# A gated hybrid decoder layer on one core: first operands loaded in another order and four pieces of work moved

## The chip, the cores and the metric

The kernel runs on one core of a Trainium2 chip, in one launch. The metric is the device time in microseconds (us), as the median of several runs; lower is better. The profile is one execution recorded by the hardware profiler. Engines: PE (TensorE) multiplies, DVE (VectorE) and ACT (ScalarE) work on elements, POOL (GpSimd) does a few small steps, SP (SyncE) issues DMA transfers.

## What is computed

One layer of a decoder, for 512 tokens of width 1024, all in float32:

```python
h  = rmsnorm(x, g_mix)
z  = h @ w_in                 # retention q,k,v,gate; 3 attention groups q,k,v; 2 merge gates
A  = silu(rg) * rmsnorm(retention(rotate(rq), rotate(rk), rv))        # 4 heads, chunks of 128
Bt = merge of 3 groups: dilated_window_attention(rotate(norm(aq)), rotate(norm(ak)), av)
x  = x + (sig(g_A) * (A @ w_ret_out) + sig(g_B) * (Bt @ w_att_out)) @ w_o
x  = x + relu(rmsnorm(x) @ w_up)**2 @ w_down
x  = x + sig(rmsnorm(x) @ w_ple_gate) * (p @ w_ple_proj)
```

The three attention groups are merged by their softmax denominators: each head's output is a sum over groups of a weight per token times the group's output.

## The kernel before, in words

**Products in three parts.** Each float32 factor is split into a high part that PE takes fast and a low part (the rest). A product is then three matmuls: high by high, high by low, low by high. The tile names carry this: `whi` and `wlo` are the parts of a weight unit, `hh` and `hl` those of the activations. `split_unit` (line 223) makes the two parts of a weight unit of 256 x 512: the high part on ACT (line 237), the rest on DVE (line 238). `mm3` (line 246) issues the three matmuls (lines 249 to 251), 128 x 128 by 128 x 512 each.

**Weights.** `make_plan` (line 1164) lists all weight units in the order of use. `fetch` issues their DMAs on SP (line 200) into six raw buffers; `ahead(n)` (line 205) fetches and splits so that n units lie ready past the used ones; `units(n)` (line 217) hands out n units and calls `ahead` for two more.

**A row projection** (`rows_gemm`, line 253) has eight k blocks of 128 channels, two weight units at a time, and four token tiles t of 128. For each t and each unit six matmuls run; then `tick` (line 115) moves a clock on by one, so a projection of 96 matmuls has 16 ticks. `later(lag, fn)` queues work that is let out `lag` ticks later, at most two entries every second tick, in the order of the queue among those that are due. So transposes, scores and merging are put between the matmuls of projections. `force(key)` lets entries out until the named one is done.

**Order of instructions.** Outside marked stretches a planner orders each engine's instructions. Within `manual_schedule` ACT and DVE keep program order: that holds for the query and key projections of the first attention group (lines 659 to 662) and for the tail. Instructions marked with `keep_in_program_order` keep theirs too. DMAs on SP are ordered by the planner everywhere.

**The start** (`setup`, line 377; `first_panel`, line 441). `x_cols` is x transposed: eight tiles of 128 channels x 512 tokens. On SP, tiles of x and of the first weights alternate (lines 388 and 391), 256 KB each. The very first weights come in two halves, one on ACT's queue and one on SP's (lines 393 and 394). The gains' columns `gcol` come first on ACT's queue (line 382). Seven matmuls on zeros warm PE up (line 411). Each x tile is scaled by its gain into `hh` on ACT (line 449) and into `hl` on DVE (line 450); the very first `whi` is made by DVE (line 233). The first k block is multiplied in rounds: for all four t high by high (line 468), then low activations (line 470), then low weights (line 472). From k = 1 on each t has its three products in a row by `mm3`. The last four k blocks run t by t, and each finished t is consumed.

**The first query projection** (`att_proj(0, 0)`, line 580, the lazy case). It runs without the norm of x; after the last t it works out the token factors, then a factor per token and head (`factor`, line 611: DVE, then a power on POOL, line 614) and multiplies the rotated tiles by it (`scale`, line 616, on DVE, line 618). `tables` (line 569) multiplies rotation rows and gains on DVE (line 573). `heads_T` (line 552) queues the transposes of the rotated tiles, one head an entry (line 559).

**Later work of interest.** After each attention group's projections, `scores`, `transpose4` and `values` are queued. After the third group `merge` (line 722) is queued: a chain of small DVE and ACT steps makes a weight for every token, group and head; the weights are gathered in `cw` (line 754), transposed on PE (line 756), copied by ACT, written to DRAM (line 760), and loaded back as rows spread over all partitions (line 766). `weigh` (line 768) multiplies each head's group output by its row (line 771) and adds (line 776); after a head's third group the sum is split into `oh` and `ol` (lines 780 and 781). The twelve steps are queued, and the mix (line 922), far behind, forces them. `ret_proj` (line 796) makes the retention keys: copy, rotation and decay per t, then `heads_T` with a lag of 9.

Of the kernel before, what the change touches and what calls it, by code (L numbers as in the profile page):

```python
# [14 lines left out]
ALU = mybir.AluOpType  # L15
AX = mybir.AxisListType

P = 128
# [58 lines left out]
class Block:  # L77
# [299 lines left out]
    def setup(self):  # L377
        nc, a = self.nc, self.a
        self.gcol = self.const.tile([P, 48], F32, name="gcol")
        xr = [self.big("xr") for _ in range(2)]  # L380
        self.x_cols = [xr[k // 4][:, k % 4] for k in range(KD)]
        nc.scalar.dma_start(self.gcol, a["vec_cols"])
        for u in range(KD // 2):
            src, _ = self.plan[u]
            raw = self.wraw.tile([P, 1024], F32, tag="raw", name=self.nm("raw")).rearrange("p (k n) -> p k n", k=2)
            for k in range(2):
                c = slice((2 * u + k) * P, (2 * u + k + 1) * P)
                nc.sync.dma_start(self.x_cols[2 * u + k], a["x_cols"][c])
                w = src[k * P : (k + 1) * P]
                if u or k:  # L390
                    nc.sync.dma_start(raw[:, k], w)
                else:
                    nc.scalar.dma_start(raw[: P // 2, k], w[: P // 2])
                    nc.sync.dma_start(raw[P // 2 :, k], w[P // 2 :])
            self.raws.append((raw, None))
        self.load_tables()
        self.fetch(6)
        self.x_tiles = []
        xb = [self.big("x") for _ in range(2)]
        for t in range(NT):  # L400
            v = xb[t // 2].rearrange("p (t c) n -> p t (c n)", t=2)[:, t % 2]
            nc.sync.dma_start(v, a["x"][0, t * P : (t + 1) * P])
            self.x_tiles.append(v)
        self.ident = self.const.tile([P, P], F32, name="ident")
        make_identity(nc, self.ident)
        warm = self.tmp("warm")
        nc.vector.memset(warm, 0.0)
        nc.scalar.activation(warm[:, 500:501], warm[:, 501:502], AF.Copy)
        wb, wps = warm.bitcast(mybir.dt.bfloat16), self.bank("warm")
        for _ in range(WARM):  # L410
            nc.tensor.matmul(wps, wb[:, :P], wb[:, :512], start=True, stop=True)
        self.mhalf = self.const.tile([P, H], F32, name="mhalf")
        nc.gpsimd.memset(self.mhalf, -0.5)
# [18 lines left out]
        self.nc.sync.dma_start(self.gains[:, g0:g1].rearrange("p g n e -> p (g n e)"),  # L432
                               bass.AP(tensor=g.tensor, offset=g.offset + w * g0, ap=[[0, P], [1, w * (g1 - g0)]]))

    def load_rest(self):
        self.nc.sync.dma_start(self.mask, self.a["c_mask"])
        self.gain_rows(1, NG)
        self.rot_rows(1)


    def first_panel(self, consume, tables):
        nc = self.nc
        self.hT = self.new_act(2, "h")
        us = []

        def split_x(k):
            g = self.gcol[:, k : k + 1]
            h, l = (part[k // 4][:, k % 4] for part in self.hT)
            self.pin(nc.scalar.activation(R(h), self.x_cols[k], AF.Copy, scale=g))
            nc.vector.scalar_tensor_tensor(R(l), self.x_cols[k], g, h, op0=ALU.mult, op1=ALU.subtract)  # L450

        self.pinned = True
        for u in range(KD // 2):
            self.hook = lambda i: split_x(2 * u + i)
            us += self.units(1)
        self.hook = None
        self.pinned = False
        banks = [self.gbank() for _ in range(NT)]

        def part(t, k):  # L460
            wh, wl = us[k // 2]
            sh, sl = self.stat(self.hT, k, t, False)
            self.mm3(banks[t], sh, sl, wh[:, k % 2], wl[:, k % 2], k == 0, k == KD - 1)

        (wh, wl), mm = us[0], nc.tensor.matmul
        parts = [self.stat(self.hT, 0, t, False) for t in range(NT)]
        for t, (sh, _) in enumerate(parts):
            mm(banks[t], sh, wh[:, 0], start=True, stop=False)
        for t, (_, sl) in enumerate(parts):
            mm(banks[t], sl, wh[:, 0], start=False, stop=False)  # L470
        for t, (sh, _) in enumerate(parts):
            mm(banks[t], sh, wl[:, 0], start=False, stop=False)
        for k in range(1, KD // 2):
            for t in range(NT):
                part(t, k)
        tables()
        self.ready_tabs = self.tables(0, 1)
        for t in range(NT):
            for k in range(KD // 2, KD):
                part(t, k)  # L480
            consume(t, banks[t])
            if t == 1:
                self.pinned = True
                self.ahead(2)
                self.pinned = False
            self.tick()
# [82 lines left out]
    def tables(self, g, n):  # L569
        C = self.tabp.tile([P, NT, HD], F32, tag="tab", name=self.nm("C"))  # L570
        Sn = self.tabp.tile([P, NT, HD], F32, tag="tab", name=self.nm("S"))
        for o, part, gi in ((C, 0, 2 * n), (Sn, 1, 2 * n + 1)):
            ins = self.nc.vector.tensor_tensor(
                o, self.rc[:, 0, :, part * HD : (part + 1) * HD],
                self.gains[:, g, gi].unsqueeze(1).to_broadcast([P, NT, HD]), op=ALU.mult)
            if g == 0:
                self.tc.keep_in_program_order(ins)
        return C, Sn

    def att_proj(self, g, n):  # L580
# [5 lines left out]
        def consume(t, ps):  # L586
            ss, v, r = self.small(H, "ss"), self.small(H, "v"), self.small(H, "r")
            j = self.tmp("j")
            for h in range(H):
                c = slice(h * HD, (h + 1) * HD)  # L590
                nc.scalar.activation(j[:, c], ps[:, c], AF.Square, accum_out=ss[:, h : h + 1])
            C, Sn = tabs[0]
            rots.append(self.rotate(ps, C[:, t], Sn[:, t]))
            sums.append((ss, v, r))
            if not lazy:
                factor(t)
                if t:
                    scale(t - 1)
                if t == NT - 1:
                    scale(t)  # L600
            elif t == NT - 2:
                self.token_squares(0)
            elif t == NT - 1:
                self.token_squares(2)
                self.token_factors()
                for i in range(NT):
                    factor(i)
                for i in range(NT):
                    scale(i)

# [45 lines left out]
    def attention(self, g):  # L656
        nc = self.nc
        if g == 0:
            with self.tc.manual_schedule(engines={nc.scalar.engine, nc.vector.engine}):
                qT = self.att_proj(g, 0)  # L660
                kT = self.att_proj(g, 1)
                self.load_rest()
        else:
            qT, kT = self.att_proj(g, 0), self.att_proj(g, 1)
        v = self.v_proj(g > 0)
        oT = self.big("oT")
        st = self.const.tile([P, NT, 2, H], F32, name=f"st{g}")

# [53 lines left out]
    def merge(self, groups, oh, ol):  # L722
# [29 lines left out]
        wide = self.tmp("cw")[:, : NG * H * NT]  # L752
        for g in range(NG):
            nc.vector.tensor_copy(wide[:, g * H * NT : (g + 1) * H * NT].rearrange("p (h r) -> p r h", h=H), cs[g])
        ps = self.bank("pc")
        nc.tensor.transpose(ps[: NG * H * NT, :P], wide, self.ident)
        turned = self.tmp("ct")[: NG * H * NT, :P]
        nc.scalar.activation(turned, ps[: NG * H * NT, :P], AF.Copy)
        cd = self.dram.tile([NG * H, S], F32, name="c_dram", tag="c_dram")
        nc.sync.dma_start(cd.rearrange("a (r l) -> (a r) l", r=DIL), turned)  # L760
        accs, spread = [None] * H, {}
        nat = lambda ap: ap.rearrange("p (l r) -> p r l", r=DIL)

# [4 lines left out]
        def weigh(h, g):  # L768
# [7 lines left out]
            nc.vector.tensor_tensor(n, accs[h], t, op=ALU.add)  # L776
            accs[h] = n
            if g == NG - 1:
                av = n.rearrange("p (r l) -> p r l", r=DIL)
                nc.scalar.activation(R(nat(oh[:, h])), av, AF.Copy)  # L780
                nc.vector.tensor_tensor(R(nat(ol[:, h])), av, nat(oh[:, h]), op=ALU.subtract)

        items = [(h, g) for h in range(H) for g in range(NG)]
        for i, (h, g) in enumerate(items):
            if i == 0:
                for p in items[:3]:
                    self.later(4, lambda p=p: load(*p))

            def step(i=i, h=h, g=g):
                weigh(h, g)  # L790
                if i + 3 < len(items):
                    load(*items[i + 3])
            self.later(8, step, ("O", h, g))


    def ret_proj(self, extra=None):
# [7 lines left out]
                extra(t, rots[t])  # L804

        self.rows_gemm(self.hT, KD, consume)
        return self.heads_T(rots, False, 9)

    def ret_cols(self):

# [111 lines left out]
    def mix(self, A, O):  # L922
        nc = self.nc
        U, Z = [[None] * 4, [None] * 4], {}
        for pair in ((0, 2), (1, 3)):
            parts = {}
            for br, act, nk, bo in (("a", O, H, 24), ("r", A, KD, 16)):
                if pair[0] and br == "r":
                    self.load_x()
                for cc in pair:  # L930
# [32 lines left out]
                    for h in range(H):  # L963
                        if br == "a":
                            self.force(("O", h, NG - 1))
                        else:
                            for i in range(NT):
                                self.force(("A", h, i))
# [216 lines left out]
    def run(self):  # L1185
# [4 lines left out]
        for g in range(NG):  # L1190
            groups.append(self.attention(g))
        oh, ol = self.big("oh"), self.big("ol")
        self.later(12, lambda: self.merge(groups, oh, ol))
        A = self.retention()
        mx = self.mix(A, ([oh], [ol]))
        self.tail(mx)
# [29 lines left out]
```

## Time and profile before

| | |
|---|---|
| Median of 3 runs | 998.5 us (998.46 to 999.19) |
| Profiled execution, its own time | 997.21 us |
| Span from first to last instruction in it | 995.4 us, so 1.8 us lie around it |
| Mean granted clock of PE | 1.000 |
| DMA in the span | 141.15 MB, 142 GB/s in the mean |

In a row of the waits stand the waiting engine with the tile it writes and its line, the releaser, the us in total, the times, and the longest. In a row of the timeline stand the start, the duration, engine, line, operation, tiles, shapes and the count of merged instructions, and in brackets the idle time before and what ended it. Matmuls are pipelined: an instruction's duration is longer than the step to the next one, so the pace is read from starts. In a DMA row stand the count, the size and the median time from issue to landing. In a row of groups stand the count, the busy time in us, the mean ns of one and the idle time before. A row of windows gives the stretch, its length, the busy time of PE, PE's weight loads, DVE, ACT and POOL, the granted clock, the DMA share and GB/s.

### The profile page before, as it was taken

The page shows a single profiled execution, that of the slowest core. Times are in us where ns is not written, and L with a number is a line of the kernel's source. Part 1 is how long each engine was busy: PE and PEld are TensorE (multiplying, and loading weights), DVE is VectorE, ACT ScalarE, POOL GpSimd, SP SyncE. Part 2 cuts the span into 40 slices and gives each one's busy share as a digit, 9 for nine tenths or more (in the row PEclk, how much of TensorE's full clock was granted, in tenths as well). Part 3 has the DMA queues.
Part 4 walks back from the last instruction along what each step waited for, and adds up shares of the span by engine and source line. Part 5 has one row for each costly group of instructions (what it writes and reads, how often), then busy time and mean ns, then how long its engine had stood idle before and what let it go on. Part 6 is the DMA issues. An engine that isn't in the chain of part 4 may idle for free.

```text
span 995.4 us, 12449 instructions
## 1 busy us (share of the span) xinstructions
PE 984.7 (99%) x4588; PEld 826.1 (83%) x4588; DVE 647.6 (65%) x1014; ACT 461.8 (46%) x938; POOL 97.4 (10%) x98
## 2 busy tenths in 40 slices
PE   8999999999999999999999999999999999999998
PEld 6788899889887888888888878888888888888886
DVE  6866675774878344554643696668667759766953
ACT  5535344433433334342422447764564565465451
POOL 0210220220000010001002010110101001000000
PEclk9999999999999999999999999999999999999999
DMA  9632132323353312222346496758659766875911
GB/s 337 240 101 76 54 106 85 105 76 106 93 142 120 113 43 85 86 85 85 132 146 166 125 233 193 190 128 225 179 136 212 203 167 153 238 160 131 312 54 53
DMA packets 90781, 141.15 MB, mean 142 GB/s; under 512 B 6320, under 2 KB 40416, under 8 KB 90720
## 3 DMA queue, kind: packets, MB, share of 16 engines
q1 hardware_dynamic: 79616, 119.22, 37.5%
q0 software_dynamic: 10880, 20.97, 12.7%
q8 instruction: 36, 0.59, 0.2%
q10 hardware_dynamic: 224, 0.16, 0.1%
q14 instruction: 25, 0.20, 0.1%
HBM read 136.10 MB, written 4.24 MB: 141 GB/s over the span
## 4 chain that ended last, share of the span: by engine, by line
PE 94%; DVE 4%; issue 1%; DMA 0%; ACT 0%; POOL 0%; ACTq 0%; DVEq 0%; POOLq 0%
PE pg L251 25%; PE pg L250 25%; PE pg L249 25%; PE pb L251 3%; PE pb L249 3%; PE pb L250 3%; PE po L700 1%; PE ph L559 1%; PE pt L325 1%; PE sc L677 1%; DVE wlo L238 1%; PE ry L899 1%; PE pe L651 1%; PE kv L887 1%; PE sc L683 1%
## 5 line engine op out<-in xcount | busy, mean ns | idle before, releaser
L238 DVE TENSOR_TENSOR wlo<-raw,whi 128x1024 fp32r<-128x1024 f32 (+1 forms) x166 | 196.8, 1191 | 103.8 <-ACT whi L237 101.8
L237 ACT ACTIVATE whi<-raw 128x1024 fp32r<-128x1024 f32 (+1 forms) x165 | 169.5, 1032 | 195.3 <-PE pg L251 75.4
L249 PE MATMUL pg<-whi,hh 128*128 128x512 f32 x444 | 178.6, 402 | 0.0
L250 PE MATMUL pg<-wlo,hh 128*128 128x512 f32 x444 | 173.6, 391 | 1.0 <-DVE wlo L238 1.0
L251 PE MATMUL pg<-whi,hl 128*128 128x512 f32 x444 | 173.7, 391 | 0.0
L250 PEld LDWEIGHTS pg<-wlo,hh 128*128 128x128 f32 x444 | 91.4, 206 | 15.3 <-DVE wlo L238 1.4
L251 PEld LDWEIGHTS pg<-whi,hl 128*128 128x128 f32 x444 | 91.1, 205 | 15.1
L249 PEld LDWEIGHTS pg<-whi,hh 128*128 128x128 f32 x444 | 91.3, 206 | 14.0
L249 PE MATMUL pg<-h2h,whi 128*128 128x512 f32 x256 | 99.6, 389 | 0.0
L250 PE MATMUL pg<-h2l,whi 128*128 128x512 f32 x256 | 99.6, 389 | 0.0
L251 PE MATMUL pg<-h2h,wlo 128*128 128x512 f32 x256 | 99.6, 389 | 0.0
L242 ACT ACTIVATE whi<-raw,gcol 128x256 fp32r<-128x256 f32 (+1 forms) x144 | 66.1, 523 | 21.3 <-PE pg L250 12.4
L243 DVE SCALAR_TENSOR_TENSOR wlo<-raw,gcol,whi 128x256 fp32r<-128x256 f32 (+1 forms) x144 | 65.5, 510 | 15.6 <-ACT whi L242 15.6
L202 POOL DMA_DIRECT2D raw<-in_w_down x32 | 38.6, 1206 | 302.4 <-DMA raw<-in_w_down 147.8
L249 PE MATMUL pg<-hh,whi 128*128 128x512 f32 x160 | 64.0, 400 | 0.0
L249 PE MATMUL pg<-whi,uh 128*128 128x512 f32 x160 | 62.8, 392 | 0.0
L251 PE MATMUL pg<-whi,ul 128*128 128x512 f32 x160 | 62.6, 392 | 0.0
L250 PE MATMUL pg<-wlo,uh 128*128 128x512 f32 x160 | 62.4, 390 | 0.0
L251 PE MATMUL pg<-hh,wlo 128*128 128x512 f32 x160 | 62.4, 390 | 0.0
L250 PE MATMUL pg<-hl,whi 128*128 128x512 f32 x160 | 62.3, 390 | 0.0
L250 PEld LDWEIGHTS pg<-h2l,whi 128*128 128x128 f32 x256 | 48.0, 188 | 10.0
L251 PEld LDWEIGHTS pg<-h2h,wlo 128*128 128x128 f32 x256 | 48.0, 188 | 10.0
(201 smaller groups left out, 1685.2 us busy)
## 6 DMA issues: line engine op xcount, KB each, us to landing
raw<-in_w_in SPq DMA_DIRECT2D x72, 512.0 KB, 4.1
raw<-in_w_down SPq DMA_DIRECT2D x48, 512.0 KB, 4.3
raw<-in_w_up SPq DMA_DIRECT2D x32, 512.0 KB, 5.2
raw<-in_w_down POOLq DMA_DIRECT2D x32, 512.0 KB, 6.7
raw<-in_w_o SPq DMA_DIRECT2D x12, 512.0 KB, 4.3
x<-in_x SPq DMA_DIRECT2D x8, 512.0 KB, 7.1
raw<-in_w_ret_out SPq DMA_DIRECT2D x8, 512.0 KB, 3.5
raw<-in_w_o POOLq DMA_DIRECT2D x8, 512.0 KB, 5.8
```

The costliest lines, as they stand in the source:

```text
L202: self.nc.gpsimd.dma_start(raw, rows(add[0]), accum_op=ALU.add)
L237: self.pin(nc.scalar.activation(R(hi[:, i]), raw[:, i], AF.Copy))
L238: nc.vector.tensor_tensor(R(lo[:, i]), raw[:, i], hi[:, i], op=ALU.subtract)
L242: self.pin(nc.scalar.activation(R(hi[:, i]), raw[:, i], AF.Copy, scale=g))
L243: nc.vector.scalar_tensor_tensor(R(lo[:, i]), raw[:, i], g, hi[:, i], op0=ALU.mult, op1=ALU.subtract)
L249: t.matmul(ps, sh, mh, start=first, stop=False, skip_group_check=more)
L250: t.matmul(ps, sh, ml, start=False, stop=False, skip_group_check=more)
L251: t.matmul(ps, sl, mh, start=False, stop=last, skip_group_check=more)
L325: nc.tensor.transpose(ps[:, k * P : (k + 1) * P], part[:, k * P : (k + 1) * P], self.ident)
L559: self.nc.tensor.transpose(ps[:, t * P : (t + 1) * P], rots[t][:, h * HD : (h + 1) * HD], self.ident)
L651: self.nc.tensor.transpose(ps[:, k * P : (k + 1) * P], e[:, k * P : (k + 1) * P], self.ident)
L677: nc.tensor.matmul(sc[:, h * P : (h + 1) * P], qT[:, h, rs], kT[:, h, rs], start=True, stop=True)
```

## The change

1. In `setup`, the first x tile is loaded in halves of 256 tokens, and the first weights come in one piece on SP between them. ACT's queue no longer carries weights.
2. In `first_panel`, the first x tile is scaled in halves; k blocks 0 and 1 are both multiplied in rounds.
3. In the lazy query projection, `ahead(4)` is called between the factors and the scalings.
4. `load_rest` goes: the mask is loaded after the first group's key projection, the other gains and the second rotation rows after its value projection.
5. `tables` keeps program order for all groups.
6. `merge` is queued with lag 20 instead of 12. In it, the transpose of the weights with the copy and the write behind it is an entry of its own four ticks later; the loads come at 6 instead of 4 and the steps at 10 instead of 8. The split of each head's sum becomes an entry four ticks behind its last step, which the mix forces as well.
7. The transposes of the retention keys have a lag of 14 instead of 9.

```diff
             for k in range(2):
                 c = slice((2 * u + k) * P, (2 * u + k + 1) * P)
-                nc.sync.dma_start(self.x_cols[2 * u + k], a["x_cols"][c])
-                w = src[k * P : (k + 1) * P]
-                if u or k:
-                    nc.sync.dma_start(raw[:, k], w)
-                else:
-                    nc.scalar.dma_start(raw[: P // 2, k], w[: P // 2])
-                    nc.sync.dma_start(raw[P // 2 :, k], w[P // 2 :])
+                first = u == 0 and k == 0
+                x = lambda i: nc.sync.dma_start(self.x_cols[2 * u + k][:, i], a["x_cols"][c, i])
+                x(slice(0, 256) if first else slice(0, S))
+                nc.sync.dma_start(raw[:, k], src[k * P : (k + 1) * P])
+                if first:
+                    x(slice(256, S))
...
-            self.pin(nc.scalar.activation(R(h), self.x_cols[k], AF.Copy, scale=g))
-            nc.vector.scalar_tensor_tensor(R(l), self.x_cols[k], g, h, op0=ALU.mult, op1=ALU.subtract)
+            for c in (slice(0, 256), slice(256, S)) if k == 0 else (slice(0, S),):
+                self.pin(nc.scalar.activation(R(h[:, c]), self.x_cols[k][:, c], AF.Copy, scale=g))
+                nc.vector.scalar_tensor_tensor(R(l[:, c]), self.x_cols[k][:, c], g, h[:, c], op0=ALU.mult, op1=ALU.subtract)
...
-        parts = [self.stat(self.hT, 0, t, False) for t in range(NT)]
-        for t, (sh, _) in enumerate(parts):
-            mm(banks[t], sh, wh[:, 0], start=True, stop=False)
...
-        for k in range(1, KD // 2):
+        for k in range(2):
+            parts = [self.stat(self.hT, k, t, False) for t in range(NT)]
+            for t, (sh, _) in enumerate(parts):
+                mm(banks[t], sh, wh[:, k], start=k == 0, stop=False)
+            for t, (_, sl) in enumerate(parts):
+                mm(banks[t], sl, wh[:, k], start=False, stop=False)
+            for t, (sh, _) in enumerate(parts):
+                mm(banks[t], sh, wl[:, k], start=False, stop=False)
+        for k in range(2, KD // 2):
...
-            if g == 0:
-                self.tc.keep_in_program_order(ins)
+            self.tc.keep_in_program_order(ins)
...
                 for i in range(NT):
                     factor(i)
+                self.ahead(4)
                 for i in range(NT):
                     scale(i)
...
-                self.load_rest()
+            self.nc.sync.dma_start(self.mask, self.a["c_mask"])
...
         v = self.v_proj(g > 0)
+        if g == 0:
+            self.gain_rows(1, NG)
+            self.rot_rows(1)
...
-        ps = self.bank("pc")
-        nc.tensor.transpose(ps[: NG * H * NT, :P], wide, self.ident)
...
+        def turn():
+            ps = self.bank("pc")
+            nc.tensor.transpose(ps[: NG * H * NT, :P], wide, self.ident)
+            turned = self.tmp("ct")[: NG * H * NT, :P]
+            nc.scalar.activation(turned, ps[: NG * H * NT, :P], AF.Copy)
+            nc.sync.dma_start(cd.rearrange("a (r l) -> (a r) l", r=DIL), turned)
+
+        self.later(4, turn)
...
+                def split():
+                    av = n.rearrange("p (r l) -> p r l", r=DIL)
+                    nc.scalar.activation(R(nat(oh[:, h])), av, AF.Copy)
+                    nc.vector.tensor_tensor(R(nat(ol[:, h])), av, nat(oh[:, h]), op=ALU.subtract)
+
+                self.later(4, split, ("split", h))
...
-                    self.later(4, lambda p=p: load(*p))
+                    self.later(6, lambda p=p: load(*p))
...
-            self.later(8, step, ("O", h, g))
+            self.later(10, step, ("O", h, g))
...
-        return self.heads_T(rots, False, 9)
+        return self.heads_T(rots, False, 14)
...
                             self.force(("O", h, NG - 1))
+                            self.force(("split", h))
...
-        self.later(12, lambda: self.merge(groups, oh, ol))
+        self.later(20, lambda: self.merge(groups, oh, ol))
```

More of the change, by code (lines that the diff above doesn't have):

```diff
@@ L433, in gain_rows @@
                                bass.AP(tensor=g.tensor, offset=g.offset + w * g0, ap=[[0, P], [1, w * (g1 - g0)]]))
[L435 to L438, printed above, removed]
     def first_panel(self, consume, tables):
@@ L465, in first_panel @@
         (wh, wl), mm = us[0], nc.tensor.matmul
-        parts = [self.stat(self.hT, 0, t, False) for t in range(NT)]
-        for t, (sh, _) in enumerate(parts):
[L468 to L472, printed above, removed]
-        for k in range(1, KD // 2):
+        for k in range(2):
[7 more added lines that the diff above has]
+        for k in range(2, KD // 2):
             for t in range(NT):
@@ L754, in merge @@
             nc.vector.tensor_copy(wide[:, g * H * NT : (g + 1) * H * NT].rearrange("p (h r) -> p r h", h=H), cs[g])
-        ps = self.bank("pc")
-        nc.tensor.transpose(ps[: NG * H * NT, :P], wide, self.ident)
-        turned = self.tmp("ct")[: NG * H * NT, :P]
-        nc.scalar.activation(turned, ps[: NG * H * NT, :P], AF.Copy)
         cd = self.dram.tile([NG * H, S], F32, name="c_dram", tag="c_dram")
-        nc.sync.dma_start(cd.rearrange("a (r l) -> (a r) l", r=DIL), turned)
+        def turn():
[5 more added lines that the diff above has]
+        self.later(4, turn)
         accs, spread = [None] * H, {}
@@ L778, in weigh @@
             if g == NG - 1:
-                av = n.rearrange("p (r l) -> p r l", r=DIL)
-                nc.scalar.activation(R(nat(oh[:, h])), av, AF.Copy)
-                nc.vector.tensor_tensor(R(nat(ol[:, h])), av, nat(oh[:, h]), op=ALU.subtract)
+                def split():
[3 more added lines that the diff above has]
+                self.later(4, split, ("split", h))
         items = [(h, g) for h in range(H) for g in range(NG)]
```

## The prediction

> **What bounds the kernel now.** I began with the page's first part, then took the waits of PE alone.
>
> ```profile
> span 995.4 us, 12449 instructions
> ...
> PE 984.7 (99%) x4588; PEld 826.1 (83%) x4588; DVE 647.6 (65%) x1014; ACT 461.8 (46%) x938; POOL 97.4 (10%) x98
> ```
> ```profile
> PE pg L468 <- DVE whi L233: 1.9, 1, 1.9
> PE warm L411 <- DVE warm L407: 1.5, 1, 1.5
> PE ph L559 <- DVE ro L549: 1.2, 1, 1.2
> PE pg L250 <- DVE wlo L238: 1.0, 1, 1.0
> PE pc L756 <- DVE cw L754: 0.8, 1, 0.8
> ```
>
> PE works in 99% of the span, so an edit pays only where PE stands still, and the second view lists every such place: the wait for the first operands and three single waits for DVE. (The warm-up's own wait comes before any data and stays.) The change touches all four; what it can win is their sum, and what it can lose is a new entry in this list. PE's starts in order of time give the size of each gap.
>
> ```profile
> 1.46 3.17 PE L411 MATMUL warm<-warm 128*128 128x512 bf16 x7 [1.46 <-DVE warm L407]
> 6.53 1.17 PE L468 MATMUL pg<-whi,hh 128*128 128x512 f32 x4 [1.90 <-DVE whi L233]
> ...
> 9.35 0.39 PE L249 MATMUL pg<-whi,hh 128*128 128x512 f32 x1
> ```
>
> The first k, twelve matmuls, takes 6.53 to 9.35: 2.82 us, 0.235 each. That is PE's pace, and whatever starts it earlier moves everything behind it.
>
> **The start.** Five views: the chain's first wait, the DMA issues and their time to landing, the queue of SP, then DVE and ACT.
>
> ```profile
> 1.19 4.74 DMA raw<-in_w_in
> ```
> ```profile
> xr<-in_x_cols SPq DMA_DIRECT2D x1, 256.0 KB, 3.0
> raw<-in_w_in SPq DMA_DIRECT2D x1, 128.0 KB, 3.1
> raw<-in_w_in ACTq DMA_DIRECT2D x1, 128.0 KB, 4.7
> gcol<-in_vec_cols ACTq DMA_DIRECT2D x1, 24.0 KB, 3.2
> ```
> ```profile
> raw<-in_w_in SPq DMA_DIRECT2D x2, 256.0 KB, 4.8
> ```
> ```profile
> 1.18 0.55 SPq L394 DMA_DIRECT2D raw<-in_w_in  x1
> 1.78 0.57 SPq L388 DMA_DIRECT2D xr<-in_x_cols  x1
> ```
> ```profile
> 5.96 0.43 DVE L233 CAST whi<-raw 128x512 fp32r<-128x512 f32 x1 [4.56 <-DMA raw<-in_w_in]
> ...
> 8.23 0.68 DVE L238 TENSOR_TENSOR wlo<-raw,whi 128x512 fp32r<-128x512 f32 x1
> ```
> ```profile
> 3.96 0.72 ACT L449 ACTIVATE hh<-xr,gcol 128x512 fp32r<-128x512 f32 x1 [0.69 <-DMA gcol<-in_vec_cols]
> 6.44 0.72 ACT L449 ACTIVATE hh<-xr,gcol 128x512 fp32r<-128x512 f32 x1 [1.76 <-DMA xr<-in_x_cols]
> 7.10 0.63 ACT L237 ACTIVATE whi<-raw 128x512 fp32r<-128x512 f32 x1
> ```
>
> The two halves of the first weights leave within 0.01 us of each other, SP's at 1.18 and ACT's at 1.19, but SP's lands after 3.1 us (4.3) and ACT's after 4.74 (5.93). DVE's cast starts at 5.96 and PE at 6.53, so the first matmul follows the last landing by 0.60 us. In the new form all the weights go on SP behind half of x. Up to their last byte SP has then moved 128 + 256 KB, the same 384 KB as 256 + 128 KB now. Lower bound of their landing: 1.18 + 3.1 = 4.3. Upper bound: the next 256 KB pieces of this queue need 4.8, which gives 6.0 and no gain. I take 4.6, near the lower end, because the row nearest in size, place and bytes ahead is the 3.1 us one; the 0.3 is for a larger transfer. The first matmul is then at 4.6 + 0.6 = 5.2, a gain of **1.3 us** (bounds 1.6 and -0.1).
>
> [...]
>
> Is anything else late at 5.2? ACT's first scaling waits until 3.96 for the gains' columns, as before, and half a tile costs at most the 0.72 of a whole one: done by 4.7. The second half of x is issued where the second x tile is now, at 1.78, with half its bytes; at 3.1 us it lands at 4.9 and is scaled by 5.6. PE wants it with the third matmul, 5.2 + 2 x 0.235 = 5.7. That is tight, with no stall in the sum; its bad case is a rival. DVE gets one more instruction, at most 0.7, behind a cast that runs 1.3 earlier. ACT's queue loses one DMA issue and SP keeps its count.
>
> The next k is wanted at 5.2 + 2.82 = 8.0. Its whi is ready at 7.10 + 0.63 = 7.73 and its wlo at 8.23 + 0.68 = 8.91, neither counted as earlier. In the old order of products wlo is the second operand wanted, at 8.2: a stall of 0.7. In rounds it is wanted eight matmuls later, at 9.9. So the rounds cost nothing and protect the gain.
>
> **The wait at 39 us.** PE, then DVE:
>
> ```profile
> 39.27 0.39 PE L249 MATMUL pg<-whi,hh 128*128 128x512 f32 x1
> 40.66 0.50 PE L250 MATMUL pg<-wlo,hh 128*128 128x512 f32 x1 [1.00 <-DVE wlo L238]
> ```
> ```profile
> 34.06 0.63 DVE L613 TENSOR_SCALAR v<-ss,floor 128x4 f32<-128x4 f32 x4
> 35.86 0.69 DVE L618 TENSOR_TENSOR ro<-ro,r 128x512 f32<-128x512 f32 x1 [1.17 <-POOL r L614]
> ...
> 39.39 3.49 DVE L238 TENSOR_TENSOR wlo<-raw,whi 128x1024 fp32r<-128x1024 f32 x3
> ```
>
> The step from 39.27 to 40.66 is 1.39 us against 0.235: 1.16 lost. DVE works in program order here; four scalings wait one by one for POOL, and the weights PE needs are split only from 39.39. With the added call two weight units (L238, 3.49/3 = 1.16 each) stand ahead of the scalings: 34.69 to 37.0, two units before PE asks. Part of that fills the 1.17 in which DVE is idle now. The scalings then find their factors made and end at about 37.0 + 4 x 0.69 = 39.8, against 39.4; their readers, the head transposes, are sixteen ticks away. Gain **1.16 us**, 0 if the raw weights were late, which ACT's split of them does not show.
>
> **The wait at 265 us.**
>
> ```profile
> 265.21 0.39 PE L251 MATMUL pg<-hh,wlo 128*128 128x512 f32 x1
> 266.37 0.27 PE L756 MATMUL pc<-ident,cw 128*48 128x128 f32 x1 [0.77 <-DVE cw L754]
> ```
>
> 1.16 less 0.235: 0.93 lost, because the transpose of the group weights is put on PE in the same tick as the DVE chain that makes its input. Four ticks of six matmuls, 4 x 6 x 0.235 = 5.6 us, now lie between them. Gain **0.93 us**, less about 0.15 for one more break in the stream of matmuls (an estimate: the first matmul after this stretch's transposes needs a load that the 0.235 pace otherwise hides).
>
> **The wait at 309 us.**
>
> ```profile
> 308.47 0.71 PE L559 MATMUL ph<-ident,ro 128*128 128x128 f32 x5
> 310.38 0.55 PE L559 MATMUL ph<-ident,ro 128*128 128x128 f32 x3 [1.20 <-DVE ro L549]
> ```
> ```profile
> L771 DVE TENSOR_TENSOR mt<-oT,cb 128x512 f32<-128x512 f32 x12 | 8.2, 696 | 0.8 <-ACT oT L151 0.8
> ...
> L781 DVE TENSOR_TENSOR ol<-mt,oh 128x512 fp32r<-128x512 f32 x4 | 4.4, 1095 | 1.4 <-ACT oh L780 1.4
> ```
> ```profile
> 312.00:334.00 22.00, 22.00 (x103) 18.30 (x102) 11.42 (x13) 8.87 (x10) 0.00 (x0) 1.00 0.34 104
> ```
>
> The last rotated tile of the retention keys is late because DVE weighs the attention groups among the rotations. I count **1.2 us**, the listed wait. The transposes move five ticks (7 us) later, and the weighing starts eight plus two ticks (14 us) later, so it leaves most of the rotations. That weighing is 8.2 + 4.4, and eight additions at about 0.7, 5.6: 18.2 us of DVE. It goes into the next projection, where the last row has DVE at 11.42 of 22. Four ticks of delay of each split have no cost: its reader, the mix, is far behind.
>
> **The small moves.** Mask, gains and rotation rows leave SP's early stretch for places where their first readers (masking of scores, tables of the second group, retention keys) are still tens of microseconds off. The tables of later groups stay in order on DVE, four products less among the early ones. Taken at nothing; if the gains were late, DVE would stop ahead of the second group's weights, bounded by one SP transfer, 4.8 us.
>
> **Sum.** 1.3 + 1.16 + 0.93 + 1.2 - 0.15 = 4.4, rounded up to 4.6 for the slow steps right behind each wait (0.50 against 0.39 at 40.66, the same at the start). The profiled execution, 997.21, becomes 992.6. It lies 1.3 under the shown median, 998.5, so the forecast is **993.9**.
>
> **Rivals.**
> - *A new wait of DVE takes the place of one removed*: order outside the written-out stretches is a planner's, and 14 us later other work crosses. Price: one wait like those listed, 1.2 to 1.4. For: three such waits stand now. Against: DVE's room in the row above. 995.2.
> - *The second half of x gates*: if it takes 4.7 to 4.8 like the later pieces, it lands at 6.5, is scaled by 7.2, and PE's third matmul starts no sooner than now. The start gains nothing: 995.3.
> - *Cold matmuls*: seven warm-up matmuls take 3.17 us, 0.45 each, and those of the same width from 6.53 on 0.235. When PE speeds up, between 4.6 and 6.5, no row shows. If at 6.5, the 1.3 us that are won run at half pace: 0.65 lost, 994.6. The page prints the granted clock at full throughout, so it doesn't tell. [...]
> - *The change does only what stands in written-out stretches*: the planner brings the waits at 265 and 309 back under other names. 998.5 - 1.3 - 1.16 = 996.0.
> - *Slower*: the weighing, pushed into the next projection, meets its weight splits. 11.42 + 18.2 = 29.6 us of DVE in 22: up to 7.6 us late, and PE waits for wlo there. This decides from 4.6 us of lateness; in full 998.5 - 4.6 + 7.6 = 1001.5. Against: part of that 11.42 is weighing already, and the weighing starts in the stretch before.
>
> **How the numbers follow.** A measurement here can tell about 0.2%, 2.0 us. Forecast 0.5; new wait 0.15; late half 0.1; cold 0.05; written-out stretches only 0.1; slower 0.1. Faster takes the first four and a third of the fifth, 0.83, of which I keep 0.79 for what the list misses. Slower: 0.07, since lateness under 4.6 falls within 0.2%; same: 0.14. The range starts at 992.8 (start at its bound, the whole 1.36 of the last wait) and goes to 997.0, past the late half with one new wait (996.6); the slower case and a little of the fifth are left out.
>
> **What would show it.** First L468 at 5.0 to 5.4, with a wait for whi under 0.8; k = 1 without a gap; no wait for L238 at 38 us, with two L238 ahead of the first L618; the turn's transpose without a wait; no wait for the rotated keys; weighing between 292 and 320. Wrong: the second-half landing ends PE's first wait; a DVE wait over 1 us in 290 to 335; a first step at 0.43.

## The result

The changed kernel takes 993.42 us (median of four runs, 993.11 to 993.8), the one before 998.79 (four runs, 998.46 to 999.19). The ratio is 0.9944, with a 95% interval of 0.993 to 0.9959: faster by 5.4 us, between 4.1 and 7.0. The forecast was 993.9.

The profile's first part and the waits of PE in the changed kernel (its line numbers are shifted a little against the kernel before, as are those of each variant):

```profile
span 991.8 us, 12456 instructions
...
PE 984.9 (99%) x4588; PEld 826.7 (83%) x4588; DVE 648.8 (65%) x1015; ACT 462.1 (47%) x939; POOL 98.1 (10%) x98
```
```profile
PE warm L410 <- DVE warm L406: 1.5, 1, 1.5
PE pb L325 <- DVE x L1026: 0.3, 1, 0.3
```

All four waits that the change aimed at are gone from the list, and one of 0.3 us, far behind, is new. PE's busy time is what it was. The span fell by 3.6 us, from 995.4 to 991.8, while the medians fell by 5.4. Followed by the same matmuls in both profiles, PE's lead over the kernel before is 0.8 us at the third block of channels, 2.1 behind the place of the wait at 39 us, 3.1 behind the one at 265 and 4.5 behind the one at 309. Some 0.4 of it is lost at 918 us, where the new wait stands, and 0.3 behind the last matmul. A single profile of each kernel doesn't give the 5.4; the experiments show where the rest is.

**The start.** PE's starts in the changed kernel, then the third block of channels in the one before:

```profile
4.74 1.71 PE L464 MATMUL pg<-whi,hh 128*128 128x512 f32 x4
6.29 1.09 PE L466 MATMUL pg<-whi,hl 128*128 128x512 f32 x4
...
8.43 1.19 PE L464 MATMUL pg<-whi,hh 128*128 128x512 f32 x4
...
11.28 0.39 PE L249 MATMUL pg<-whi,hh 128*128 128x512 f32 x1
```
```profile
12.07 0.39 PE L249 MATMUL pg<-whi,hh 128*128 128x512 f32 x1
```

The first matmul begins at 4.74 instead of 6.53, 1.8 us earlier, yet the third block begins only 0.8 us earlier (11.28 against 12.07). Half a microsecond goes in the first four matmuls, which take 1.71 instead of 1.17. Another 0.3 goes where the second block waits (its first matmul could start at about 8.1), and 0.1 in the slow step behind that wait. DMA and ACT show what was late:

```profile
xr<-in_x_cols SPq DMA_DIRECT2D x2, 128.0 KB, 2.5
raw<-in_w_in SPq DMA_DIRECT2D x1, 256.0 KB, 3.0
```
```profile
4.55 0.51 ACT L444 ACTIVATE hh<-xr,gcol 128x256 fp32r<-128x256 f32 x1 [0.97 <-DMA xr<-in_x_cols]
5.81 0.72 ACT L444 ACTIVATE hh<-xr,gcol 128x512 fp32r<-128x512 f32 x1 [0.74 <-DMA xr<-in_x_cols]
7.75 0.63 ACT L237 ACTIVATE whi<-raw 128x512 fp32r<-128x512 f32 x1 [1.21 <-DMA raw<-in_w_in]
```

The first weights in one piece land after 3.0 us, the two half tiles of x after 2.5 in the median. The second half of x is scaled by 4.55 + 0.51 = 5.06, before the third matmul starts (the first three start at 4.74, 5.30 and 5.73), so the slow first matmuls don't wait for it: their steps of 0.56 and 0.43 us are those of a slower clock, and the trace's record of the clock begins its full-speed stretch only at 5.92 us. After the second x tile, ACT idles 1.21 us for the weights of the second block, and their high part is ready at 7.75 + 0.63 = 8.38; before, it was ready at 7.73.

**The other three places.** DVE around the scalings, PE's transpose of the group weights, and the retention keys' transposes:

```profile
33.07 2.36 DVE L238 TENSOR_TENSOR wlo<-raw,whi 128x1024 fp32r<-128x1024 f32 x2
35.35 0.69 DVE L614 TENSOR_TENSOR ro<-ro,r 128x512 f32<-128x512 f32 x1
```
```profile
L753 DVE COPY cw<-c x3: 173/176/177, 271.0 to 271.1; 128x16 f32<-128x16 f32 x3
...
L758 PE MATMUL pc<-ident,cw x1: 270/270/270, 283.5 to 283.5; 128*48 128x128 f32 x1
```
```profile
310.85 1.04 PE L555 MATMUL ph<-ident,ro 128*128 128x128 f32 x8
```
```profile
312.00:334.00 22.00, 22.00 (x103) 18.29 (x102) 13.94 (x17) 10.20 (x12) 0.00 (x0) 1.00 0.37 121
```

Two splits stand ahead of the scalings. The group weights are there 12 us before PE turns them (271.1 and 283.5). Eight key transposes run in one piece. In the window PE is busy without a break, and DVE rose from 11.42 to only 13.94 of 22, so the weighing that the slower rival feared found room.

### The profile page after: what moved, and what is told of

Same layout as the page of the kernel before. It is cut to its first block, busy times and chain, and to the rows that moved or that the text cites. A ratio compares the mean times of both kernels' runs of the same rounds, so it can differ in the third digit from the quotient of the medians.

```text
span 991.8 us, 12456 instructions
## 1 busy us (share of the span) xinstructions
PE 984.9 (99%) x4588; PEld 826.7 (83%) x4588; DVE 648.8 (65%) x1015; ACT 462.1 (47%) x939; POOL 98.1 (10%) x98
## 4 chain that ended last, share of the span: by engine, by line
PE 97%; DVE 1%; ACT 1%; DMA 1%; SPq 0%; issue 0%; ACTq 0%; DVEq 0%
PE pg L249 27%; PE pg L251 27%; PE pg L250 27%; PE pb L251 3%; PE pb L250 3%; PE pb L249 3%; PE po L699 1%; PE ph L555 1%; PE pt L325 1%; PE sc L676 1%; PE ry L905 1%; PE pe L647 1%; PE kv L893 1%; PE sc L682 1%; PE ry L907 1%; DMA raw<-in_w_in 1%
## 5 line engine op out<-in xcount | busy, mean ns | idle before, releaser
L249 PEld LDWEIGHTS pg<-h2h,whi 128*128 128x128 f32 x256 | 48.1, 188 | 9.9
```

What stands on the lines that cost most here:

```text
L249: t.matmul(ps, sh, mh, start=first, stop=False, skip_group_check=more)
```

## The experiments

Each group of four was run on one chip beside the kernel before. The medians of before in the three groups are 998.48 (27 runs, 996.38 to 1000.17), 998.25 (16 runs, 996.54 to 999.88) and 998.34 us (9 runs, 996.78 to 999.7).

**The change in its parts.** `start_only` is the kernel before with items 1 and 2 of the change. `no_start` is the changed kernel without them. `scale_only` is the kernel before with this line:

```diff
                     factor(i)
+                self.ahead(4)
                 for i in range(NT):
                     scale(i)
```

`merge_lag_only` is the kernel before with items 6 and 7:

```diff
-        self.later(12, lambda: self.merge(groups, oh, ol))
+        self.later(20, lambda: self.merge(groups, oh, ol))
...
+        self.later(4, turn)
...
-        return self.heads_T(rots, False, 9)
+        return self.heads_T(rots, False, 14)
```

> The kernel before with the new start alone (x in halves, first weights in one piece, two rounds). Theory: every wait of PE that goes is worth its own length. In the profiles PE reaches the third block of channels 0.8 us earlier, so 0.8 us faster, 998.0. Rival: the timed executions of before are 1.3 to 1.6 us slower than its profiled one, and that is the start too (the moment at which PE's clock opens), so the new start is worth about 2 us: 996.8.

> The changed kernel with the old start. Theory: 0.8 us slower than the changed one, 994.2; first matmul at 6.5 us, no wait at 39, 265 and 309 us. Rival that the start is worth 2 us: 995.4.

> The kernel before with the call that splits two weight units ahead of the four scalings, alone. Theory: the wait of 1.0 us for wlo at 40.7 us goes, with the slow step behind it 1.3 us faster, 997.5. Rival: it comes back as a wait for the rotated query heads at 51 us, because the scalings end later: no change, 998.8.

> The kernel before with the new lags alone (merge at 20, transposing, splitting and loading later, key heads at 14). Theory: the waits for cw and for the rotated keys go, 1.0 + 1.4 us faster: 996.4. Rival: without the new order of tables and of the mask, gain and rotation loads the planner brings a wait back: under 1 us faster, 998.

| kernel | median us (range) | ratio to before, 95% interval |
|---|---|---|
| start_only | 996.3 (995.84 to 996.65) | 0.998 (0.9971 to 0.9989) |
| no_start | 994.08 (993.64 to 995.41) | 0.9962 (0.995 to 0.9974) |
| scale_only | 997.59 (996.17 to 999.38) | 0.9997 (0.9988 to 1.0006) |
| merge_lag_only | 996.05 (994.49 to 997.66) | 0.9976 (0.9967 to 0.9985) |

The medians fall by 2.2, 0.9 and 2.4 us for the three parts, 5.5 together: they add up to the 5.4 of the whole, though the ranges are wide enough that this alone proves little (`new_again`, below, puts the whole at 4.6). `scale_only` alone is too small for its interval, and its wait shows it instead. The waits of PE in `start_only`, then in `scale_only`:

```profile
PE warm L410 <- DVE warm L406: 1.5, 1, 1.5
PE ph L560 <- DVE ro L550: 1.2, 1, 1.2
PE pg L250 <- DVE wlo L238: 1.0, 1, 1.0
PE pc L757 <- DVE cw L755: 0.8, 1, 0.8
PE pg L469 <- DVE whi L233: 0.3, 1, 0.3
```
```profile
PE pg L468 <- DVE whi L233: 1.9, 1, 1.9
PE warm L411 <- DVE warm L407: 1.5, 1, 1.5
PE ph L559 <- DVE ro L549: 1.2, 1, 1.2
PE pc L757 <- DVE cw L755: 0.8, 1, 0.8
```

Each part takes its own waits off the list and leaves the others with their lengths; of the first wait `start_only` keeps 0.3 us. The rivals fall: no wait moved to the query heads at 51 us, and `merge_lag_only` lost both of its waits without items 4 and 5, which weren't tried by themselves. Its own two items, 6 and 7, weren't tried apart either.

For the start the two measurements differ: 2.2 us by `start_only`, some 0.5 to 0.7 by `no_start` against the changed kernel. And the kernel before spreads over nearly 4 us, `start_only` over less than 1. The times of before fall into two groups: of the 27, six lie at 996.38 to 997.08 and the others at 997.9 and above. PE in the profile of `merge_lag_only`, which has the old start, suggests why:

```profile
1.46 3.17 PE L411 MATMUL warm<-warm 128*128 128x512 bf16 x7 [1.46 <-DVE warm L407]
5.95 2.05 PE L468 MATMUL pg<-whi,hh 128*128 128x512 f32 x4 [1.32 <-DVE whi L233]
7.79 1.80 PE L470 MATMUL pg<-whi,hl 128*128 128x512 f32 x4
9.43 1.09 PE L472 MATMUL pg<-wlo,hh 128*128 128x512 f32 x4
10.36 0.40 PE L249 MATMUL pg<-whi,hh 128*128 128x512 f32 x1
```

Here eight matmuls run at about half pace (5.95 to 9.43: 0.435 each), and the first block takes 4.41 us instead of the 2.82 of before's profile, which happened to show the good case. So a theory of the clock: after the warm-up PE idles for more than a microsecond, and in some executions its clock then stays at half for some us more (here for about 3.5, from 5.95 on).

The traces keep a record of the clock, and for the profiled executions it bears this out. Its full-speed stretch begins at 4.7 to 4.8 us in `before`, `scale_only` and `no_start`, right behind the warm-up, and all their matmuls run at full pace. It begins at 9.3 us in `merge_lag_only`, where the pace changes. The times agree with this: the profiled execution of `no_start`, 993.79, is one of its three faster ones (993.64 to 994.08; the other two took 995.29 and 995.41).

The same explains in part why the two measurements of the start differ: three of the five runs of `no_start` look like executions with the good case. And in its profile the third block starts 0.65 us later than in the changed kernel, but the last matmul only 0.23 later, because `no_start` doesn't have the wait at 918 us.

**The clock.** `new_again` is the changed kernel unaltered. The others:

```diff
-WARM = 7
+WARM = 11      # old_warm11, in the kernel before
+WARM = 3       # new_warm3, in the changed kernel
+WARM = 8       # new_early_warm, in the changed kernel, with the lines below
-        nc.vector.memset(warm, 0.0)
-        nc.scalar.activation(warm[:, 500:501], warm[:, 501:502], AF.Copy)
+        nc.vector.memset(warm[:, :256], 0.0)
+        nc.scalar.activation(warm[:, 300:301], warm[:, 201:202], AF.Copy)
```

> The changed kernel once more, unaltered, as the measure for its variants on the same chip: 993.4. Theory of the clock (below) expects all its executions within 1 us, since PE's work begins 0.1 to 0.3 us after the warm-up and leaves no gap in which the clock could stay shut; the kernel before spreads over some 3 us.

> The kernel before with eleven warm-up matmuls instead of seven, so that PE has work up to about 6.2 us and its first real matmul at 5.9 to 6.5 is not held back. Theory: in some executions of before PE's gap from 4.6 to 6.5 us keeps the clock shut for another three or four us (first block of channels at half pace, 1.6 us more); with the gap filled these go, the median falls by 1 to 1.5 us to about 997.3 and the slowest executions with it. Rival: the spread of before comes from the landing of the first weights, not from the clock: median and spread as before, 998.5.

> The changed kernel with three warm-up matmuls: PE idles from about 2.9 to 4.7 us, as long as before, but earlier. Theory of the clock: the first matmuls run at 0.43 us each until 7 to 10 us in every execution, 1 to 2 us slower, 994.4 to 995.4. Rival without the clock: 993.4.

> The changed kernel with half of the warm-up tile cleared, so that PE's warm-up begins about 0.25 us earlier, and eight warm-up matmuls, which end where seven ended. Theory: the clock opens at the same time or earlier, 0 to 0.5 us faster than the changed kernel, 993.0 to 993.4. Rival: the eighth matmul holds the first real one back, 0.2 us slower.

| kernel | median us (range) | ratio to before, 95% interval |
|---|---|---|
| new_again | 993.63 (993.03 to 994.02) | 0.9956 (0.9943 to 0.9968) |
| old_warm11 | 996.7 (996.21 to 997.49) | 0.9986 (0.9977 to 0.9995) |
| new_warm3 | 994.85 (994.31 to 995.29) | 0.9971 (0.9959 to 0.9982) |
| new_early_warm | 993.7 (992.82 to 993.75) | 0.9956 (0.9943 to 0.9968) |

Four more warm-up matmuls make the old kernel 1.55 us faster, and its range shrinks from 3.3 to 1.3 us, though nothing in its loads was changed: most of the spread was the clock's, not the landing's. Four fewer make the new one 1.2 us slower. The first block in `old_warm11`, then in `new_warm3`:

```profile
1.46 4.87 PE L411 MATMUL warm<-warm 128*128 128x512 bf16 x11 [1.46 <-DVE warm L407]
6.29 1.57 PE L468 MATMUL pg<-whi,hh 128*128 128x512 f32 x4
...
9.51 0.39 PE L249 MATMUL pg<-whi,hh 128*128 128x512 f32 x1
```
```profile
4.77 2.05 PE L464 MATMUL pg<-whi,hh 128*128 128x512 f32 x4 [1.85 <-DVE whi L233]
6.61 1.91 PE L466 MATMUL pg<-whi,hl 128*128 128x512 f32 x4
8.32 1.78 PE L468 MATMUL pg<-wlo,hh 128*128 128x512 f32 x4
```

With three, the twelve matmuls of the block run at about half pace, 0.43 us each, and the clock's record opens at 9.8 us. With eleven, PE works without a long gap from 1.46 us on, yet the record opens only at 7.15, so the first four matmuls still take 1.57 instead of 1.17 and the block 3.2 us, between the 2.82 and the 4.41 above. Beginning 0.27 us earlier (`new_early_warm`) changes nothing that these runs can tell.

**The start in its pieces.** All four are variants of the changed kernel. `one_round` multiplies only the first block in rounds. `x_whole` loads and scales the first x tile whole, the weights behind it. `w_two_queues` splits the first weights over both queues again, with x still in halves. `halves_two` does with the second x tile what the change does with the first. Of the edits only the main lines of the loads are shown; the scalings follow them. Where the expectations speak of the cap, they mean the theory that a landing is set by the bytes ahead of it in the queue.

```diff
-                first = u == 0 and k == 0
+                first = u == 0                      # halves_two
-                x(slice(0, 256) if first else slice(0, S))
+                x(slice(0, S))                      # x_whole
-                nc.sync.dma_start(raw[:, k], src[k * P : (k + 1) * P])
+                if first:                           # w_two_queues
+                    nc.scalar.dma_start(raw[: P // 2, k], w[: P // 2])
+                    nc.sync.dma_start(raw[P // 2 :, k], w[P // 2 :])
```

> The changed kernel with rounds for the first 128 channels only; the second 128 run tile by tile with the low weights second, as before. In the changed kernel's profile whi of the second block is ready at 8.4 us and wlo at 9.1. Theory: the second matmul of that block waits for wlo, 0.4 us, the third block begins 0.4 later, 0.4 us slower: 993.9. Rival: the wait is hidden by a later one, no change: 993.5.

> The changed kernel with the first x tile loaded and scaled in one piece, weights in one piece behind it. Theory of the cap: the first matmul comes 0.3 to 0.5 us later (5.0 to 5.2), but the second block of channels waits for its weights until 8.4 us either way, because the bytes up to them are the same; the halves are worth nothing: 993.5. Rival: what the first matmul loses is lost to the end: 993.9 to 994.0.

> The changed kernel with the first weights in two halves again, one on ACT's queue and one on SP's, x in halves. Theory: the ACT half lands at 5.0 to 5.9 us as before the change, the first matmul is at 5.6 to 6.5, the second block begins at 8.5 to 9.2, and a gap behind the warm-up leaves the clock shut in some executions: 0.3 to 1.5 us slower, 994 to 995, with a wider spread. Rival: two queues serve no worse than one, 993.5.

> The changed kernel with the second x tile in halves too, its weights between them, and on ACT the second half scaled behind the weights' high part. Theory of the cap: the second block's weights land with 128 KB less ahead of them, 0.3 to 0.5 us earlier, and the block begins at 7.9 to 8.1 instead of 8.4 to 8.6; 0.3 to 0.5 us faster than the changed kernel, 993.0. Rival: the second half of x is then the gate, or landings there go by time and not by bytes: no change, 993.5.

| kernel | median us (range) | ratio to before, 95% interval |
|---|---|---|
| one_round | 993.82 (993.33 to 993.99) | 0.9955 (0.9943 to 0.9968) |
| x_whole | 992.49 (992.1 to 993.17) | 0.9944 (0.9932 to 0.9956) |
| w_two_queues | 994.5 (993.02 to 994.99) | 0.9959 (0.9946 to 0.9973) |
| halves_two | 992.46 (992.2 to 993.09) | 0.9945 (0.9931 to 0.9959) |

`one_round` has the expected wait, and its third block begins at 11.54 instead of 11.28, but 0.3 us can't be told in the median. PE:

```profile
8.18 0.49 PE L249 MATMUL pg<-whi,hh 128*128 128x512 f32 x1 [0.27 <-ACT whi L237]
8.91 0.50 PE L250 MATMUL pg<-wlo,hh 128*128 128x512 f32 x1 [0.23 <-DVE wlo L238]
```

`w_two_queues` brings the late landing back, on both queues, and with it the gap and, in this profile, the half pace (the clock's record opens at 9.5 us); its range is the widest of the four, and its median is 0.9 us above `new_again`, with overlapping intervals. Its DMA rows and PE:

```profile
raw<-in_w_in ACTq DMA_DIRECT2D x1, 128.0 KB, 3.7
raw<-in_w_in SPq DMA_DIRECT2D x1, 128.0 KB, 3.9
```
```profile
5.74 2.05 PE L469 MATMUL pg<-whi,hh 128*128 128x512 f32 x4 [1.11 <-DVE whi L233]
```

`x_whole` was expected to cost nothing or 0.5; its median is a microsecond below the changed kernel's instead. ACT's high part of the second block's weights, and PE:

```profile
6.44 0.63 ACT L237 ACTIVATE whi<-raw 128x512 fp32r<-128x512 f32 x1 [0.17 <-DMA raw<-in_w_in]
```
```profile
4.87 1.35 PE L461 MATMUL pg<-whi,hh 128*128 128x512 f32 x4 [0.25 <-DVE whi L233]
...
7.90 1.07 PE L461 MATMUL pg<-whi,hh 128*128 128x512 f32 x4
...
10.62 0.39 PE L249 MATMUL pg<-whi,hh 128*128 128x512 f32 x1
```

The expectation that equal bytes land at equal times doesn't hold in these profiles: the second block's weights come at 6.4 here and at 7.7 in the changed kernel, with the same bytes ahead of them and one transfer fewer. Half a microsecond of that is the issue itself: SP issues them at 2.11 here and, behind one more transfer, at 2.59 there. The first matmul is 0.13 later and the third block 0.66 earlier. But `start_only`, with the same transfers as the changed kernel, shows its second block without a wait too, and `new_again`, the changed kernel itself, shows a longer one:

```profile
7.96 1.07 PE L469 MATMUL pg<-whi,hh 128*128 128x512 f32 x4
```
```profile
PE pg L464 <- ACT whi L237: 0.9, 1, 0.9
```

So this landing varies between executions, and one profile each doesn't show that whole tiles land sooner. The medians favour `x_whole` and `halves_two` (third block at 10.52) by about 1 us, but the changed kernel wasn't run beside them on that chip, the intervals of the ratios overlap, and the ratio of `x_whole` to before is the 0.9944 that the changed kernel had. Part of the difference lies behind 570 us: PE's lead over the changed kernel in the profile of `x_whole` is 0.7 us at the third block and 1.4 at the last matmul. In the changed kernel DVE stands 0.47 us between two steps at 918 us, and PE waits for it; in `x_whole` it doesn't:

```profile
918.26 0.75 DVE L1026 SCALAR_TENSOR_TENSOR x<-pb,f,x 128x512 f32<-128x512 f32 x1 [0.47 <-DVE x L1026]
```
```profile
916.84 0.75 DVE L1023 SCALAR_TENSOR_TENSOR x<-pb,f,x 128x512 f32<-128x512 f32 x1
```

Why is open. PE's wait for it came in both profiles of the changed kernel (here, `new_again`) and in `new_warm3`, `new_early_warm` and `one_round`, not in `x_whole`, `halves_two`, `w_two_queues` and `no_start`. By their medians `x_whole` and `halves_two` are the best kernels of the study, below both that were given.

## Why the prediction was right

**The waits.** All four went, as the likeliest case had it, and the three behind the start came back nowhere; the one new wait in the list, 0.3 us at 918 us, is a quarter of the size that the rival of a new wait was given. The one at 39 us was put at 1.16, those at 265 and 309 us at 0.93 and 1.2, less 0.15. That 0.15 was an estimate for one more break in the stream; in the changed profile the matmul behind the moved transpose steps 0.32 (283.53 to 283.85) and the next one 0.24, so about 0.1 of it shows. By PE's lead in the two profiles the three were worth 1.3, 1.0 and 1.4. `scale_only` lost the first and no other; `merge_lag_only` lost the other two for 2.4 us in its median. Five ticks and eight plus two were ample: the group weights lay ready for 12 us.

**The start, where a step failed.** The term of 1.3 us was 0.8 in the profiles. The first matmul at 4.74 is better than the 5.2 of the sum; the weights landed at the lower bound (after 3.0 us). But the step "its whi is ready at 7.73, neither counted as earlier" failed: the weights of the second block landed later than before, their high part was ready at 8.38, and the block waited, 0.3 us in this profile and 0.9 in that of `new_again`. Two signs failed with it: the first matmul came before 5.0, and the second block had the gap that was to be absent. I had followed the transfer that got faster and not the ones behind it in the same queue.

**The clock, a rival that turned round.** It was priced as a loss of 0.65 us. The loss is there: 0.5 us in the first four matmuls of the changed profile, and the sign of being wrong that I had named, a first step at 0.43, came in the second step (0.56, then 0.43). But I had priced it against the one profile of before, in which the clock happened to be open at 6.53 (its record has full speed from 4.8 us on). In the timed runs of before, which leave no trace, it often was not, by the evidence of `old_warm11`, which puts this at 1.55 us. So the start is worth more in the medians (2.2 by `start_only`) than the two profiles show (0.8). The sum of 4.6 against the measured 5.4 misses that. The warning was in the table: the profiled execution lay 1.3 us under the median, and I carried the difference along as a constant instead of asking which part of the kernel varies. The `no_start` runs, only 0.5 to 0.7 us slower than the changed kernel, don't show the same value; five runs don't settle it.

So the mechanism of the waits was right, and that the number is right to 0.5 us is partly luck. Between the two profiled executions the change is 3.7 us (997.21 to 993.55), 0.9 less than the sum; the medians moved 1.7 us more than that, about what the clock is worth by `old_warm11`, and the sum had no term for it. The lower end of the range, 992.8, doesn't follow from the terms named for it either: 0.3 for the start at its bound and 0.16 for the last wait lead from 993.9 to 993.4, and there the median came to lie.

The time from the first warm-up matmul to full speed was not the same in the profiles. By the record of the clock it was 3.1 us in one (`new_again`, whose first four matmuls take 1.17 from 4.67 on) and 4.5 us in the other one of the same kernel. It was 5.7 us in `old_warm11`, which left PE no long gap, and 7.9 us in `merge_lag_only`.

```profile
4.67 1.17 PE L464 MATMUL pg<-whi,hh 128*128 128x512 f32 x4
```

**Queues.** The first weights landed at the lower end of the range: after 3.0 us in one piece on one queue, against 3.7 and 3.9 in two (`w_two_queues`). I had taken ACT's half for the late one, as in the profile of before (4.7 us, SP's 3.1). In `no_start` it was SP's half that came late (4.5 us, ACT's 3.6), and in `merge_lag_only` neither came early (4.0 and 4.2). What holds a half back no run shows.

**The small moves did not happen.** I had the mask, gains and rotation rows leave SP's early stretch. SP in the changed kernel:

```profile
17.34 0.33 SPq L658 DMA_DIRECT2D mg<-in_c_mask  x1
...
23.27 0.37 SPq L427 DMA_DIRECT2D rotc<-in_c_rot  x1
```

Though they are written tens of microseconds later, the planner issues them where it did before: the mask at 17.3 us (16.95 in the kernel before), the second gains at 19.4 (19.1), the second rotation rows at 23.3 (23.0). Taken at nothing, they were nothing, but for another reason.

**The rivals.** The second half of x did not gate the first block: a wait for its scaling is in no list of PE's waits. The slower case stayed away: DVE had 8 of 22 us to spare where the weighing went.

## What to carry to other kernels

Where PE is busy 99% of the time, list its waits one by one: each that was moved out of the way here was worth about its length, they added up, and the list of waits showed it even where the median couldn't. At the start of a kernel ask not only when the first matmul runs but whether PE has work without a gap from its warm-up on, and follow the transfers behind the one that was hurried. When a single profile lies off the median by more than the effect, find out first what differs between executions.

## What the runs showed of the hardware

After a warm-up of 3.2 us and a gap of 1.1 us or more, the next matmuls ran at half pace (0.43 us each) for about 3.5 us in two profiles (`merge_lag_only`, `w_two_queues`) and at full pace at once in three (`before`, `scale_only`, `no_start`); eleven warm-up matmuls in place of seven narrowed the range of the times from 3.3 to 1.3 us. In the traces' record of the clock the full-speed stretch began at 9.3 and 9.5 us in the two and at 4.7 to 4.8 in the three. The granted clock in the views doesn't tell: in the window of `merge_lag_only` with eight matmuls at half pace its column, behind the busy times, reads 1.00, so the pace must be read from the starts.

```profile
5.95:9.43 3.48, 3.48 (x8) 2.77 (x9) 2.47 (x5) 2.09 (x4) 0.00 (x0) 1.00 1.01 354
```

The same 256 KB of weights, with equal bytes ahead of them in one queue, landed 1.3 us apart (6.4 and 7.7 us) in two profiles with different pieces ahead of them; 0.5 us of it lay in the issue (2.11 and 2.59 us). With the pieces of the later one, `start_only` began its second block at 7.96 without a wait.
